# A retention and RWKV-7 backbone on one core: a second home for the retention heads' queries, values, decays and states

## The chip, the cores and the metric

The kernel runs on one core of one Trainium2 chip. What counts is the device time of one execution in microseconds, the median of several runs. The core has five engines that each take their instructions in a fixed order: TensorE (PE in the rows, its weight loads PEld), VectorE (DVE), ScalarE (ACT), GpSimd (POOL) and SyncE (SP), on whose queue this kernel issues its DMAs.

## What is computed

Two layers over 1024 latent and 256 context tokens of width 1024. Each layer normalises the tokens, makes one input projection, and splits its columns between eight retention heads and eight RWKV-7 heads of width 64. Both groups scan the tokens in both directions; the outputs are gated, joined, sent through one output projection and added to the residual. Cut to the retention heads, which the change touches:

```python
def retention_scan(q, k, v, log_gamma, s0):          # chunks of 128 tokens
    def step(s, qkv):
        qc, kc, vc = qkv
        scores = jnp.einsum('bhid,bhjd->bhij', qc, kc) * decay_mask
        inner = jnp.einsum('bhij,bhjd->bhid', scores, vc)
        cross = jnp.einsum('bhid,bhde->bhie', qc * q_decay, s)
        s_new = s * chunk_decay + jnp.einsum('bhjd,bhje->bhde', kc * k_decay, vc)
        return s_new, inner + cross
...
    mix_l = jnp.concatenate([ret_l * silu(gr_l), rwo_l * silu(gw_l)], axis=-1) @ w_out[layer]
```

## The kernel before

The 1280 tokens are ten tiles of 128 (`NT`). Heads are worked on in pairs, so there are four pairs (`NP`) of retention heads and four of RWKV heads in each of the two layers.

The RWKV heads set the pace. For each pair and each of ten steps, `prep` loads features from DRAM, `prep2` builds the small matrices of the step (L962 and L1001 to L1040), and `seq` carries the state on (L1053, L1061). `prep` runs `LOOK` = 3 steps and one ahead. `seq` and `prep2` are traced with high priority. The RWKV results of two tiles go through `readout`.

Everything else is filler, written as generators that yield after each piece of work, with its weight. `stream()` goes over the pairs. For pair p it merges `ret_out(p - 1)`, the retention output of the pair before, with `feats(p)`: the RWKV gates of pair p and the RWKV features of pair p + 1. Then come `ret_keys(p)` and `ret_states(p)`. For the last pair (3) there are no further features, and `ret_keys(3)` is itself part of `feats(3)`; so `ret_states(3)` follows on `ret_out(2)` directly. `out_stream()` then merges `ret_out(3)` with the retention gates of pair 3 and a first part of the output projection (`out_part`), and goes on with the second part, which needs the retention output of pair 3. After each step of the scan `deal` takes as much filler as a plan of weights (`DENSE`, `DUE`) says. This gives a program order. From it the compiler's planner makes the order on each engine: an instruction may be put ahead of earlier ones where its inputs, its buffers and its engine are free by the planner's estimate of times.

A projection (`project_steps`) goes over blocks of up to 512 tokens. For each block it takes one of two PSUM banks (`pj=2`), runs 24 products into it (L493 to L495, three for each of eight slices of the width, with weights and inputs split into two halves of 16 bits), and hands the bank to a sink that copies it out on ScalarE.

`ret_states(p)` projects the values (sink at L555: copies to tiles of the ring `ta`, five in all, transposes through the bank `fs`, copy to `vt` at L563), computes the decays `dec` (L581) and the mask `dmask` (L584, its inputs in the ring `tb`, four tiles), and projects the queries (sink at L551: copy to `qt` at L552, then the rotation `rope`, which also uses `ta`). Beside the queries it computes for each tile the state that it adds (`states`, in the single bank `rt`, L589 to L597) and copies it to `sbp` (L602), and then scans these (L618). For pairs 0 to 2 the retention gates follow (`ret_gates`, stored to `rgat_d` at L623). `ret_out(p)` then reads, tile pair by tile pair, in the bank `rt`: keys and queries (L638), queries and states (L641), mask (L643), decays (L644, L645), values (L648). Its `tail` normalises, loads the gates (L666) and stores the result to `mix_d`, which `mix_in` reads for the output projection (L809).

`qt`, `vt`, `dec`, `dmask` and the ten `sbp` tiles exist once in the pool `ret`: pair p writes them after pair p - 1 has read them. The keys `kt` of pairs 0 to 2 exist once too (`rk`); those of pair 3 lie in another pool (`pk`).

Of the kernel before, what the change touches and what calls it, by code (L numbers as in the profile page):

```python
# [10 lines left out]
F32 = mybir.dt.float32  # L11
# [11 lines left out]
TOK = SEQ + CTX  # L23
NT = TOK // 128
# [101 lines left out]
def hybrid_kernel(ctx: ExitStack, tc: tile.TileContext, a: dict, out: bass.AP, dbg: dict | None = None):  # L126
    nc = tc.nc
# [11 lines left out]
    def bank(tag, name):  # L139
        return ps.tile([128, 512], F32, tag=tag, name=name, bufs=BANKS[tag])  # L140
# [24 lines left out]
    def x_tile(tb):  # L165
        t = ln_pool.tile([128, D], F32, tag="xt", name="xt", bufs=XTB)
        load(t, a["ctx"][0, 128 * tb:128 * tb + 128, :] if tb < 2 else a["x"][0, 128 * (tb - 2):128 * (tb - 2) + 128, :])
        return t
# [86 lines left out]
    def t256(name, ring="ta"):  # L255
        pool = open_pools["ret"][1] if ring == "tb" else pre
        return pool.tile([128, 256], F32, tag=ring, name=name, bufs=dict(ta=TAB, tb=TBB)[ring])
# [76 lines left out]
            halves.append((hi, lo))  # L334
        return halves

    sbp = []
    SIDES = ("left", "right")


# [33 lines left out]
    for l in range(DEPTH):  # L374
# [55 lines left out]
        if l == 0:  # L430
            lp = ln_pool
            stage = [lp.tile([128, 8, 128 * len(tiles)], F32, name=f"xs{ci}") for ci, tiles in enumerate(LN_TILES)]
            for ci, tiles in enumerate(LN_TILES):
# [5 lines left out]
                for i, tb in enumerate(tiles):  # L439
                    t = x_tiles[tb] if tb < XTB else x_tile(tb)  # L440
# [40 lines left out]
        def project_steps(c0, pieces, sink):  # L481
            halves = w_block(w_in, c0)
            for piece in pieces:
                t0, t1 = piece[0], piece[1]
                m0, m1 = piece[2:] if len(piece) == 4 else (t0, t1)
                p = pj("pproj")
                n = m1 - m0
                for hf in range(2):
                    hi, lo = halves[hf]
                    for k in range(4):  # L490
                        kk = 4 * hf + k
                        first, stop = kk == 0, kk == 7
                        nc.tensor.matmul(p[:, 0:n], hi[:, k, :], h_hi[:, kk, m0:m1], start=first, stop=False)  # L493
                        nc.tensor.matmul(p[:, 0:n], hi[:, k, :], h_lo[:, kk, m0:m1], start=False, stop=False)  # L494
                        nc.tensor.matmul(p[:, 0:n], lo[:, k, :], h_hi[:, kk, m0:m1], start=False, stop=stop)  # L495
                sink(p, m0, t0, t1)
                yield 24 * (m1 - m0) / 2400
# [25 lines left out]
        def rope(x, t0, t1):  # L523
            if t0 < CTX:
                return
            for u in range(t0, t1, 256):
                cs, sn, sw = t256("ropec"), t256("ropes"), t256("rsw")
                load(cs, a["c_cos"][:, u - CTX:u - CTX + 256])
                load(sn, a["c_sin"][:, u - CTX:u - CTX + 256])
                xs = x[:, u - t0:u - t0 + 256]  # L530
                nc.vector.stream_shuffle(sw, xs, [(i + 16) % 32 for i in range(32)])
                nc.gpsimd.tensor_tensor(sw, sw, sn, ALU.mult)
                nc.vector.tensor_tensor(xs, xs, cs, ALU.mult)
                nc.vector.tensor_tensor(xs, xs, sw, ALU.add)
# [10 lines left out]

        def ret_states(rp, c):
            sp, kt = open_pools["ret"][1], c["kt"]
            qt = c["qt"] = sp.tile([128, TOK], F32, tag="qt", name="qt")
            vt = c["vt"] = sp.tile([128, NT, 128], F32, tag="vtk", name="vtk")

            def qsink(p, m0, t0, t1):  # L551
                nc.scalar.activation(qt[:, t0:t1], p[:, 0:t1 - t0], AF.Copy, scale=1.0 / WS)  # L552
                rope(qt[:, t0:t1], t0, t1)

            def vsink(p, m0, t0, t1):  # L555
                vch = [t256("vch") for _ in range(0, t1 - t0, 256)]
                for u, x in enumerate(vch):
                    nc.scalar.activation(x, p[:, 256 * u:256 * u + 256], AF.Copy, scale=1.0 / WS)
                p = bank("fs", "pvv")
                for u, x in enumerate(vch):  # L560
                    for j in range(2):
                        nc.tensor.transpose(p[:, 256 * u + 128 * j:256 * u + 128 * j + 128], x[:, 128 * j:128 * j + 128], ident)
                nc.scalar.copy(vt[:, t0 // 128:t1 // 128, :].rearrange("p g c -> p (g c)"), p[:, 0:t1 - t0])  # L563

            yield from project_steps(COL_V + 128 * rp, CHUNKS, vsink)


            dec = c["dec"] = sp.tile([128, 2, 2, 2], F32, tag="dec", name="dec")
            cd = sp.tile([128, 2], F32, tag="cd", name="cd")
            dmask = c["dmask"] = sp.tile([128, 2, 128], F32, tag="dmk", name="dmask")  # L570
            for d in range(2):
                nc.scalar.activation(cd[:, d:d + 1], lgc[:, 4 * d + rp:4 * d + rp + 1], AF.Exp, scale=128.0)
            rel, tri = [t256(nm, "tb").rearrange("p (d t) -> p d t", d=2) for nm in ("rel", "tri")]
            load(rel, a["c_rel"][:, 0:2])
            load(tri, a["c_rel"][:, 2:4])
            for hh in range(2):
                t2 = t256("dmt", "tb").rearrange("p (d t) -> p d t", d=2)
                for d in range(2):
                    col = lgb[:, 8 * d + 2 * rp + hh:8 * d + 2 * rp + hh + 1]
                    for w in range(2):  # L580
                        nc.scalar.activation(dec[:, w, d, hh:hh + 1], kdix[:, 2 * w + d:2 * w + d + 1], AF.Exp, scale=col)  # L581
                    nc.scalar.activation(t2[:, d, :], rel[:, d, :], AF.Exp, scale=col)
                nc.vector.tensor_tensor(t2, t2, tri, ALU.mult)
                nc.vector.tensor_tensor(dmask[:, hh, :], t2[:, 0, :], t2[:, 1, :], ALU.add)  # L584


            def states(j):
                pk = bank("rt", "pkt")
                nc.tensor.transpose(pk[:, 0:128], kt[:, 128 * j:128 * j + 128], ident)  # L589
                kk = t256("kkd", "tb").rearrange("p (d c) -> p d c", d=2)  # L590
                for d in range(2):
                    nc.vector.tensor_tensor(kk[:, d, :].rearrange("p (h c) -> p h c", h=2),
                                            pk[:, 0:128].rearrange("p (h c) -> p h c", h=2),
                                            dec[:, 0, d, :].unsqueeze(2).to_broadcast([128, 2, 64]), ALU.mult)
                for d in range(2):
                    for hh in range(2):
                        nc.tensor.matmul(pk[64 * hh:64 * hh + 64, 128 + 64 * d:192 + 64 * d], kk[:, d, 64 * hh:64 * hh + 64],  # L597
                                         vt[:, j, 64 * hh:64 * hh + 64], start=True, stop=True)
                for d in range(2):
                    i = order[d].index(j)  # L600
                    if i + 1 < NT:
                        nc.scalar.copy(sbp[order[d][i + 1]][:, 64 * d:64 * d + 64], pk[:, 128 + 64 * d:192 + 64 * d])  # L602

            def own_states():
                for j in range(NT):
                    states(j)
                    yield 0.43

            def queries():
                yield from project_steps(COL_Q + 128 * rp, lat_chunks, qsink)  # L610
                if rp < NP - 1:
                    yield from ret_gates(rp)

            yield from merge(own_states(), 4.3, queries(), 26)
            for d in range(2):
                for i in range(2, NT):
                    x = sbp[order[d][i]][:, 64 * d:64 * d + 64]
                    nc.vector.scalar_tensor_tensor(x, sbp[order[d][i - 1]][:, 64 * d:64 * d + 64], cd[:, d:d + 1], x,  # L618
                                                   ALU.mult, ALU.add)

        def ret_gates(rp):
            def gsink(p, m0, t0, t1):
                load(rgat_d[:, t0:t1], gate_of(p))  # L623

            yield from project_steps(COL_G + 128 * rp, [(128 * j, 128 * j + 256) for j in out_tiles[::2]], gsink)

        def ret_out(rp, c, pairs):
            sp = open_pools["ret"][1]
            kt, qt, vt, dec, dmask = [c[x] for x in ("kt", "qt", "vt", "dec", "dmask")]

            def inner(j0, hh, ob):

# [603 lines left out]
        sp = open_pool("scan", other)  # L1236
        make_rings(sp)
        rp = open_pool("ret", other)
        sbp[:] = [rp.tile([128, 128], F32, name=f"sbp{j}") for j in range(NT)]
        for j in range(NT):  # L1240
            nc.gpsimd.memset(sbp[j], 0.0)
        stages, late = {}, {}

        def ahead(g):
# [71 lines left out]
```

## Time and profile before

| | |
|---|---|
| median of 3 runs | 2458.19 us (2457.12 to 2461.14) |
| the profiled execution | 2462.74 us |
| its span, first to last instruction | 2460.7 us |
| mean granted TensorE clock | 0.964 of 2.4 GHz |
| TensorE busy | 2299.2 us (93%) |
| TensorE weight loads | 1739.9 us (71%) |
| VectorE, ScalarE, GpSimd busy | 1735.6, 1414.8, 1319.7 us |

Rows of the profile have the form: line of the kernel, engine, operation, output tile <- input tiles, shapes, count. Times are microseconds from the start of the span. The profile has views by line, by stretch of time, of waits, and in order of time. Matmuls are pipelined, so a busy TensorE isn't one at its peak.

### The profile page before, as it was taken

What the parts mean: (1) busy time and instruction counts of PE and PEld (TensorE: products, weight loads), DVE (VectorE), ACT (ScalarE), POOL (GpSimd) and SP (SyncE); (2) the same over time, 40 slices, a digit from 0 to 9 for tenths busy, and PEclk for the clock granted to TensorE, in tenths of its full rate; (3) what the DMA queues carried; (4) which work ended last, traced back from release to release, by engine and by line L of the source; (5) the groups of instructions that cost most, each with busy time, mean ns of one, the idle gap of its engine ahead of it and who ended that gap; (6) DMA issues with size and microseconds to landing.
All of it is one profiled execution on the core that took longest, in us unless ns stands there. A gap on an engine that the chain in (4) does not pass through costs nothing.

```text
span 2460.7 us, 69593 instructions
## 1 busy us (share of the span) xinstructions
PE 2299.2 (93%) x25463; PEld 1739.9 (71%) x25463; DVE 1735.6 (71%) x4784; ACT 1414.8 (57%) x4261; POOL 1319.7 (54%) x2032
## 2 busy tenths in 40 slices
PE   5779999999999999999997899999999999998997
PEld 2357776877788777778655687778768877776855
DVE  2646686787678867777648677767867886669756
ACT  3455664565566655456546666646655665456663
POOL 1455564465556654456536556545654665456662
PEclk7888999999999999999998899999999999999998
DMA  8754443334334423335533543434433443334544
GB/s 313 270 187 110 117 118 87 113 108 124 78 89 139 126 70 92 75 100 154 176 108 123 152 130 112 108 94 119 128 87 100 124 124 80 79 88 120 143 130 128
DMA packets 539606, 302.77 MB, mean 123 GB/s; under 512 B 238995, under 2 KB 526465, under 8 KB 537217
## 3 DMA queue, kind: packets, MB, share of 16 engines
q1 hardware_dynamic: 539264, 298.33, 42.1%
q8 instruction: 201, 3.29, 0.6%
q14 instruction: 141, 1.15, 0.2%
HBM read 212.21 MB, written 85.98 MB: 121 GB/s over the span
## 4 chain that ended last, share of the span: by engine, by line
PE 58%; DVE 13%; DMA 6%; ACT 4%; issue 3%; POOL 2%; SPq 2%; DVEq 0%; POOLq 0%; ACTq 0%
PE pproj L493 8%; PE pproj L495 8%; PE pproj L494 8%; PE pseq L1061 8%; PE pm L962 5%; DMA ft<-feat 2%; PE pseq L1053 2%; PE pinv L1001 2%; PE pinv L1017 2%; PE pout L821 1%; PE pout L823 1%; PE pss L638 1%; PE pout L822 1%; PE pss L648 1%; PE pyt L1127 1%
## 5 line engine op out<-in xcount | busy, mean ns | idle before, releaser
L493 PE MATMUL pproj<-h_hi,whi 128*128 128x256 f16 (+2 forms) x2128 | 631.3, 298 | 9.1 <-ACT craw L505 5.1
L494 PE MATMUL pproj<-h_lo,whi 128*128 128x256 f16 (+2 forms) x2128 | 629.1, 297 | 7.6 <-DVE h_lo L365 7.1
L495 PE MATMUL pproj<-h_hi,wlo 128*128 128x256 f16 (+2 forms) x2128 | 627.2, 297 | 0.7 <-POOL wlo L320 0.7
L320 POOL TENSOR_TENSOR wlo<-wraw,whi 128x256 f16<-128x256 f32 x360 | 250.5, 707 | 208.7 <-ACT wraw L319 181.0
L495 PEld LDWEIGHTS <-wlo 128*128 128x128 f16 x2128 | 213.5, 100 | 76.5 <-issue 12.1
L494 PEld LDWEIGHTS <-whi 128*128 128x128 f16 x2128 | 212.6, 100 | 77.6 <-issue 18.6
L493 PEld LDWEIGHTS <-whi 128*128 128x128 f16 x2128 | 213.1, 100 | 75.3 <-issue 10.4
L986 POOL COPY ttb<-tt 64x256 f16<-64x256 f16 x320 | 139.1, 436 | 205.2 <-DVE tt L1021 160.5
L1015 DVE TENSOR_TENSOR xx<-pinv,lvm 128x256 f16<-128x256 f32 x400 | 164.3, 416 | 90.6 <-PE pinv L1001 87.4
L318 ACT ACTIVATE whi<-wraw 128x256 f16<-128x256 f32 x360 | 139.2, 412 | 132.9 <-PE pproj L494 61.1
L1018 ACT CAST tz<-pinv 128x256 f16<-128x256 f32 x400 | 146.1, 370 | 119.9 <-PE pinv L1017 107.7
L962 PE MATMUL pm<-own,bk 64*128 64x128 f32 (+1 forms) x1280 | 201.6, 294 | 8.3 <-DVE bk L942 4.0
L1021 DVE STREAM_TRANSPOSE tt<-tz 128x256 f16<-128x256 f16 x320 | 139.4, 437 | 97.0 <-ACT tz L1018 94.3
L976 POOL TENSOR_TENSOR il<-gq,c_id 64x256 f32<-64x256 f32 x160 | 120.1, 751 | 133.1 <-DVE gq L965 119.3
L986 ACT COPY ttb<-tt 64x256 f16<-64x256 f16 x320 | 128.6, 402 | 106.5 <-DVE tt L1021 102.1
L962 PEld LDWEIGHTS pm<-own,bk 64*128 64x128 f32 x1280 | 163.2, 193 | 33.1 <-issue 8.6
L965 DVE TENSOR_TENSOR gq<-pm,c_m 128x256 f32<-128x256 f32 (+1 forms) x320 | 115.7, 402 | 50.6 <-PE pm L962 49.8
L1061 PE MATMUL pseq<-st,own 64*64 64x64 f32 x2432 | 149.4, 228 | 0.0
L319 ACT ACTIVATE wraw<-wraw 128x256 f32<-128x256 f32 x376 | 146.3, 410 | 3.9
L1001 PEld LDWEIGHTS <-hi 128*128 128x128 f16 x1920 | 104.6, 99 | 41.6 <-issue 9.7
L1012 POOL TENSOR_TENSOR lo<-il,hi 64x256 f16<-64x256 f32 x160 | 113.5, 710 | 36.8 <-ACT hi L977 28.0
L1008 POOL TENSOR_TENSOR ttb<-hi,lvm 128x256 f16<-128x256 f16 x160 | 113.6, 729 | 19.0 <-ACT hi L977 18.2
(255 smaller groups left out, 5906.7 us busy)
## 6 DMA issues: line engine op xcount, KB each, us to landing
ft<-feat SPq DMA_DIRECT2D x320, 160.0 KB
wraw<-in_w_in_dram SPq DMA_DIRECT2D x264, 128.0 KB
feat<-zth SPq DMA_DIRECT2D x80, 256.0 KB
wm<-in_w_mod_dram SPq DMA_DIRECT2D x16, 1024.0 KB
wraw<-in_w_out_dram SPq DMA_DIRECT2D x112, 128.0 KB
lap<-la SPq DMA_DIRECT2D x40, 256.0 KB
uv<-vt SPq DMA_DIRECT2D x320, 32.0 KB
wm<-in_w_mod_dram SPq DMA_DIRECT2D x16, 512.0 KB
```

The source lines that it names most:

```text
L319: nc.scalar.activation(raw, raw, AF.Copy, scale=WS)
L320: nc.gpsimd.tensor_tensor(lo, raw, hi, ALU.subtract)
L493: nc.tensor.matmul(p[:, 0:n], hi[:, k, :], h_hi[:, kk, m0:m1], start=first, stop=False)
L494: nc.tensor.matmul(p[:, 0:n], hi[:, k, :], h_lo[:, kk, m0:m1], start=False, stop=False)
L495: nc.tensor.matmul(p[:, 0:n], lo[:, k, :], h_hi[:, kk, m0:m1], start=False, stop=stop)
L962: nc.tensor.matmul(pm[h][:, i, d, 0:q1], bk[HR[h], i, d, :], own[HR[h], i, d, 0:q1], start=True, stop=True)
L986: eng(idr(dst[HR[h], :, :, 64 * h:64 * h + 64]), idr(src[HR[h]]))
L1001: nc.tensor.matmul(q[:, i, d, :], hi[:, i, d, :], id16 if n == 0 else tz[:, i, d, :], start=True, stop=True)
L1015: nc.vector.tensor_tensor(xx, q, mk, ALU.mult)
L1018: nc.scalar.copy(tzn, tp)
L1021: nc.vector.transpose(idr(tt), idr(tzn))
L1061: rm = nc.tensor.matmul(pq[HR[h], k, d, :], lhs, rhs, start=False, stop=stop, skip_group_check=True)
```

## The change

Queries, values, decays and mask get two buffers each, so that the pairs take them in turn. The ten state tiles are made twice, all twenty are set to zero at the start of a layer, and pair p uses set p % 2; `ret_out` gets its pair's set through the pair's dictionary `c`. Keys, the banks, the rings and the order in which the work is traced stay as they are.

```diff
-    sbp = []
+    sbps = []
...
-            qt = c["qt"] = sp.tile([128, TOK], F32, tag="qt", name="qt")
-            vt = c["vt"] = sp.tile([128, NT, 128], F32, tag="vtk", name="vtk")
+
+            sbp = c["sbp"] = sbps[rp % 2]
+            qt = c["qt"] = sp.tile([128, TOK], F32, tag="qt", name="qt", bufs=2)
+            vt = c["vt"] = sp.tile([128, NT, 128], F32, tag="vtk", name="vtk", bufs=2)
...
-            dec = c["dec"] = sp.tile([128, 2, 2, 2], F32, tag="dec", name="dec")
+            dec = c["dec"] = sp.tile([128, 2, 2, 2], F32, tag="dec", name="dec", bufs=2)
             cd = sp.tile([128, 2], F32, tag="cd", name="cd")
-            dmask = c["dmask"] = sp.tile([128, 2, 128], F32, tag="dmk", name="dmask")
+            dmask = c["dmask"] = sp.tile([128, 2, 128], F32, tag="dmk", name="dmask", bufs=2)
...
-            kt, qt, vt, dec, dmask = [c[x] for x in ("kt", "qt", "vt", "dec", "dmask")]
+            kt, qt, vt, dec, dmask, sbp = [c[x] for x in ("kt", "qt", "vt", "dec", "dmask", "sbp")]
...
-        sbp[:] = [rp.tile([128, 128], F32, name=f"sbp{j}") for j in range(NT)]
-        for j in range(NT):
-            nc.gpsimd.memset(sbp[j], 0.0)
+        sbps[:] = [[rp.tile([128, 128], F32, name=f"sbp{n}{j}") for j in range(NT)] for n in range(2)]
+        for t in sbps[0] + sbps[1]:
+            nc.gpsimd.memset(t, 0.0)
```

## Rows read from the trace of the kernel before

**Rows 1.** The page: busy time of each engine, and the chain's shares by engine.
```profile
PE 2299.2 (93%) x25463; PEld 1739.9 (71%) x25463; DVE 1735.6 (71%) x4784; ACT 1414.8 (57%) x4261; POOL 1319.7 (54%) x2032
...
PE 58%; DVE 13%; DMA 6%; ACT 4%; issue 3%; POOL 2%; SPq 2%; DVEq 0%; POOLq 0%; ACTq 0%
```

**Rows 2.** L493 alone by window: length, busy and count, clock, DMA share, GB/s.
```profile
1000.00:1019.50 19.50, 5.90 (x18) 1.76 (x18) 1.00 0.36 89
1020.40:1053.90 33.50, 0.00 (x0) 0.00 (x0) 0.75 0.28 74
...
2181.40:2198.70 17.30, 0.07 (x1) 0.00 (x0) 0.76 0.30 77
...
2211.50:2227.50 16.00, 0.00 (x0) 0.16 (x1) 0.70 0.39 104
```

**Rows 3.** All engines by window: PE, PEld, DVE, ACT, POOL, granted clock, DMA.
```profile
1020.40:1036.80 16.40, 14.67 (x212) 12.28 (x210) 14.36 (x47) 9.28 (x27) 8.77 (x14) 1.00 0.36 93
1036.80:1057.30 20.50, 20.05 (x156) 15.52 (x157) 11.57 (x32) 8.73 (x32) 7.66 (x13) 0.50 0.16 46
2181.60:2190.50 8.90, 7.31 (x100) 6.05 (x99) 7.17 (x20) 5.15 (x14) 7.17 (x12) 1.00 0.29 77
2190.50:2200.80 10.30, 10.14 (x95) 8.56 (x95) 7.88 (x31) 5.19 (x16) 3.37 (x7) 0.50 0.30 75
2211.60:2217.80 6.20, 4.83 (x63) 3.82 (x61) 5.74 (x21) 4.12 (x12) 2.65 (x4) 1.00 0.50 157
2217.80:2228.10 10.30, 6.59 (x72) 4.88 (x69) 10.13 (x30) 4.36 (x16) 5.74 (x8) 0.50 0.34 78
```

**Rows 4.** ScalarE in order of time: start, length, instruction, idle before it.
```profile
1050.51 0.38 ACT L552 ACTIVATE qt<-pproj 128x256 f32<-128x256 f32 x1 [2.12 <-PE pss L641]
...
1061.96 0.37 ACT L563 COPY vtk<-pvv 128x256 f32<-128x256 f32 x1
...
2196.84 0.60 ACT L552 ACTIVATE qt<-pproj 128x512 f32<-128x512 f32 x1 [1.73 <-PE pss L641]
...
2220.97 0.38 ACT L686 ACTIVATE gth<-pproj 128x256 f32<-128x256 f32 x1 [0.41 <-DVE qt L533]
```

**Rows 5.** TensorE in order of time, around the same places.
```profile
1020.46 0.38 PE L495 MATMUL pproj<-h_hi,wlo 128*128 128x512 f16 x1
...
1049.42 1.06 PE L641 MATMUL pss<-sbp,qt 64*128 64x128 f32 x4
...
1053.99 0.61 PE L493 MATMUL pproj<-h_hi,whi 128*128 128x512 f16 x1
...
1061.29 0.64 PE L648 MATMUL pss<-vtk,smk 128*128 128x64 f32 x4
...
2181.52 0.38 PE L495 MATMUL pproj<-h_hi,wlo 128*128 128x512 f16 x1
...
2195.75 1.06 PE L641 MATMUL pss<-sbp,qt 64*128 64x128 f32 x4
```

**Rows 6.** Pairs 0 and 1 of layer 0, in order of time.
```profile
570.99 0.61 PE L641 MATMUL pss<-sbp,qt 64*128 64x128 f32 x4
...
635.72 0.38 ACT L552 ACTIVATE qt<-pproj 128x256 f32<-128x256 f32 x1
```

**Rows 7.** GpSimd in order of time, at the start of each layer's scan.
```profile
149.94 1.50 POOL L1241 MEMSET sbp<- 128x128 f32 x8
...
1299.16 1.54 POOL L1241 MEMSET sbp<- 128x128 f32 x10 [4.67 <-PE pout L823]
```

**Rows 8.** SyncE's DMA issues in order of time: gate reads, gate store, first mix load.
```profile
1031.35 0.58 SPq L666 DMA_DIRECT2D rmx<-rgat  x1
...
1049.36 0.53 SPq L666 DMA_DIRECT2D rmx<-rgat  x1
...
2242.40 0.38 SPq L623 DMA_DIRECT2D rgat<-gs  x1
2242.88 2.30 SPq L809 DMA_DIRECT2D mraw<-mix  x5
```

## The prediction

> **What bounds the kernel now.** I read the page's busy line and its chain first [rows 1]. In both TensorE leads: 93% of the span in its row, 58% of the chain, with the three product lines of the projections (L493, L494, L495) at the head of the chain's list. The other engines lie at 54 to 71%. So the kernel ends when TensorE has got through its work, and the question for any edit is whether TensorE is at some point short of work, or slow, because of what the edit touches.
>
> What TensorE does is of two kinds. The RWKV chain (`prep2` and `seq`) is a row of short, dependent products. The filler is projections and output products, dealt between the chain's steps. So I next asked for the filler alone: L493, the first of each three products, window by window [rows 2]. Ordinarily 18 of them start in 19.5 us. In three places none do: 33.5 us in layer 0 (1020.4 to 1053.9), 17.3 us in layer 1 (2181.4 on; the one that is counted is the end of an earlier one), and 16.0 us a little later (2211.5 on). In the whole of these windows only the RWKV chain and the retention output run.
>
> Third, all engines in the same places with the granted clock [rows 3]. In layer 0 the clock is still 1.00 in the first 16.4 us without filler, then 0.50 (1.2 instead of 2.4 GHz) for 20.5 us, until just after the filler is back. In layer 1 it is 0.50 for 10.3 us twice, again in the two lulls. Together 41.1 us at the lower level. TensorE's idle time in these windows is 16.40 - 14.67 + 20.50 - 20.05 = 2.2 us in layer 0, and 1.59 + 0.16 + 1.37 + 3.71 = 6.8 us in layer 1.
>
> The page "Perfetto Trace Analysis" of the Trainium skill (Identifying the Most-Contended Engine) says that the matmul busy share is a bad measure of what TensorE has left. The trace agrees: the row with 20.05 of 20.50 us busy holds 156 matmuls, the 16.40 us ahead of it 212 [rows 3]. By the busy share alone the lulls hold 9.0 us; with the clock it is three times that.
>
> Last, who ends the lulls [rows 4, 5]. In layer 0 the last product of the second query block of pair 3 starts at 1020.46. ScalarE copies the pair's query blocks out of PSUM (L552) only at 1050.51, and its idle time is put down to `PE pss L641`, the last product that reads the queries of pair 2 (1049.42 + 1.06 us). Two blocks wait so, and the projections have two PSUM banks (`pj=2`): no projection can start. L493 is back at 1053.99. For the values it is the same: last reader L648 at 1061.29, first copy L563 at 1061.96. In layer 1: the last query product at 2181.52, the reader at 2195.75, the copy at 2196.84. The second lull of layer 1 follows from that: the first gate block is taken up (L686) only at 2220.97, behind a `DVE qt L533`, the rotation of the late queries.
>
> It happens only with pair 3 of each layer. For pairs 1 and 2 `ret_keys` lies between (pair 3 does its keys earlier): the last read of pair 0's queries is at 570.99, pair 1's copy at 635.72, 64 us later with nothing waiting [rows 6]. Pair 2 is alike.
>
> **The change, part by part.**
>
> Queries, two homes: takes the wait of L552 away. Pair 3 takes the home that pair 1 left long ago. The two banks come free as soon as their products end (the later one at about 1021) instead of at 1051. What can then follow is the third query block (layer 0 only) and the gates of pair 3, five blocks in layer 0, four in layer 1: 6 x 8 = 48 and 4 x 8 = 32 products on L493. At the usual 18 in 19.5 us they would last 52 and 35 us; many are 256 columns wide and not 512, so half of that is the lower bound: 26 to 52 us for a lull of 33.5, and 17 to 35 us for lulls of 33.3 together.
>
> Values, two homes: L563 needn't wait for L648. Alone it opens little (the five value tiles in front of it find room), but it frees the `ta` tiles that the query rotation and the gates need next.
>
> What that is worth: the busy time at half clock would halve, (20.05 + 10.14 + 6.59) / 2 = 18.4 us, and the idle time is 9.0 us: 27.4 us at most. At least nothing, if the hole only moves. I take two thirds, 18.3 us, since the filler just about covers the lulls. What is late next: the first loads for the output products (L809, 2242.88) start right behind the last gate store (2242.40) [rows 8], so they too come forward, until they meet the end of `ret_out` of pair 2.
>
> States, decays and mask, two homes: nothing. States of the next pair can't start before `ret_out` of the last pair is done, for both use the one `rt` bank in turn, and the mask's inputs turn in the shared `tb` tiles. Only a few ScalarE exponentials on single columns (L581) may come earlier; they hide beside TensorE.
>
> Ten more memsets on GpSimd per layer: ten took 1.54 us in a row in layer 1, and eight 1.50 us in layer 0 [rows 7], so 1.5 us each layer. Behind them are `zth` and the normalisation of layer 1. Zero if hidden, 3.0 us if not; I take 1.5.
>
> The planner orders all instructions anew by its own estimates of time, and the pool grows by 16.4 KB per partition (5,120 bytes each for queries, values and states, 1,056 for mask and decays). What a new order costs elsewhere no row of before shows. The nearest are the lulls themselves: one more or one less like the shorter ones is 10.14 / 2 + 1.6 = 6.7 us either way. I take zero and keep both ends for the range.
>
> Sum: -18.3 + 1.5 = -17 us. The profiled execution took 2462.7 us (2460.7 of span and 2.0 around it), so 2446 for its like; the median of the three runs lies 4.5 us lower, at 2458.19. Forecast: 2441.
>
> **The rivals.**
>
> The clock stays low anyway. It doesn't fall for want of filler; or the moved filler is spread so thinly that it falls all the same. For it: in the half-clock stretch TensorE is already busy 20.05 of 20.50 us. Against: in three lulls of three the clock falls within the lull and is back with the filler. Then only idle time comes back, 9.0 x 2/3 - 3.0 = 3 us: 2455 (2450 to 2458). The page "TensorE: Matmul & The Clock Gate" of the Trainium skill (Part 1: The HAM clock gate) ties the lower clock to an idle engine; by that rule the lull of layer 0, busy in its row, would not be its cause. The rows bear it out only in part.
>
> The hole moves. Filler that is spent at 1020 to 1054 is missing later, ahead of the last output part, which needs the retention output of pair 3, and that isn't earlier. Then the same lull comes once more, and with memsets it is 2458 to 2461; I write 2460. Against: RWKV steps run ahead in a lull, so only their last stretch is lost.
>
> Slower, by SyncE's queue. The gates' stores (L623) overwrite the ranges that `ret_out` of pair 2 still reads (L666). Brought forward, a store must wait for its read, and behind it on SyncE's queue are `ft` and `uv`, the loads of the next RWKV step. The reads are 18 us apart (1031.35, 1049.36) [rows 8]. If the planner takes these reads for earlier than they are, one such wait per layer that outlasts the steps prepared ahead costs up to 18 us; half of it, in a layer or spread over both, makes 2458 + 9, so 2468 with the memsets. It decides when a wait outlasts the steps that are prepared ahead (LOOK is 3). Against: that is a long cover.
>
> Better than the forecast: lulls gone entirely, and the output parts packed more tightly: below 2431.
>
> **How the numbers follow.** Forecast 2441 with 2431 to 2449: 0.52. Better: 0.06. Clock stays low: 0.14. Hole moves: 0.12. Slower: 0.16. About 0.2% is what can be told from no change (2453.3 to 2463.1). Faster by more: 0.52 + 0.06 + 0.06 of the second = 0.64. Within: 0.08 + 0.10 = 0.18. Slower: 0.02 + 0.16 = 0.18. The range goes from 2428 to 2468: it takes in the slower rival's price and one spare lull below the forecast.
>
> **What would show it.** Right: L552 of pair 3 within 2 us of its products in both layers; L493 present in each 20 us between 1000 and 1075 and between 2160 and 2220; no half clock there; the first output products some 20 us earlier against the RWKV steps. The memsets show as 20 of L1241's kind a layer. Wrong, if L552 is prompt and a stretch of half clock stands somewhere else in the same layer, or if `ft` lands late behind an L623 store.

## The result: slower by 0.8%

| | before | after |
|---|---|---|
| median of 6 runs each | 2462.86 us (2457.12 to 2466.58) | 2482.76 us (2474.55 to 2489.18) |
| the profiled execution | 2462.74 us | 2484.52 us |
| its span | 2460.7 us | 2482.7 us |
| mean granted TensorE clock | 0.964 | 0.958 |
| time at the lower clock, summed over the span | 178.0 us | 210.4 us |
| TensorE busy | 2299.2 us | 2318.0 us |

The ratio is 1.008 [1.0055, 1.0104]: the change costs 20 us. The forecast was 2441, the range ended at 2468. TensorE executes the same 25463 matmuls and counts as busy 18.8 us longer; it spends 32.4 us more at the lower clock. Both are of one execution each, and neither is the price of the change, as two kernels further down show.

The page after, busy line and chain by engine, against [rows 1]. Below, lines of the kernel after carry numbers two higher than before, from L552 (now L554) on.

```profile
PE 2318.0 (93%) x25463; PEld 1750.8 (71%) x25463; DVE 1715.1 (69%) x4784; ACT 1419.2 (57%) x4261; POOL 1327.1 (53%) x2052
...
PE 68%; DVE 10%; DMA 5%; ACT 4%; issue 3%; POOL 2%; SPq 1%; DVEq 0%; POOLq 0%; ACTq 0%
```

**What the change was to do, it did.** ScalarE after, in order of time, against [rows 4]: the value copy of pair 3, its three query copies in layer 0 and the two in layer 1.

```profile
983.87 0.37 ACT L565 COPY vtk<-pvv 128x256 f32<-128x256 f32 x1 [0.67 <-PE pvv L564]
1007.29 0.38 ACT L554 ACTIVATE qt<-pproj 128x256 f32<-128x256 f32 x1 [0.60 <-PE pproj L495]
1019.86 0.60 ACT L554 ACTIVATE qt<-pproj 128x512 f32<-128x512 f32 x1
1030.05 0.58 ACT L554 ACTIVATE qt<-pproj 128x512 f32<-128x512 f32 x1
...
2187.69 0.60 ACT L554 ACTIVATE qt<-pproj 128x512 f32<-128x512 f32 x1 [0.42 <-PE pproj L495]
2196.71 0.58 ACT L554 ACTIVATE qt<-pproj 128x512 f32<-128x512 f32 x1
```

None of these copies has a read of pair 2's queries (`pss`) as its releaser any more, and the first one of layer 0 is 43 us earlier than 1050.51. L493 alone in the same places, against [rows 2] (length, busy and count, weight loads, clock, DMA share, GB/s):

```profile
1000.00:1020.00 20.00, 5.22 (x16) 1.62 (x16) 1.00 0.40 99
1020.00:1068.50 48.50, 13.24 (x47) 4.55 (x46) 1.00 0.36 93
1069.50:1180.00 110.50, 0.00 (x0) 0.00 (x0) 0.91 0.46 123
2181.40:2198.70 17.30, 6.22 (x18) 1.67 (x18) 1.00 0.43 108
2198.80:2222.50 23.70, 6.89 (x26) 2.59 (x26) 1.00 0.31 87
```

The lulls are gone, and the clock is 1.00 where it was 0.75, 0.76 and 0.70. The third row says what became of it: the layer's projections are used up by 1068.9, where before they last until 1095.7. From then on the output part is the only filler, beside the retention work itself.

**Where it was given back.** First, right behind. The output part starts at 1071.0 instead of 1098.2, and as slowly as before (there 9 of the first of each three products in its first 17 us). The first of each three output products after, by window:

```profile
1069.50:1094.70 25.20, 3.04 (x8) 1.12 (x9) 0.66 0.43 123
```

Second, ahead of the second output part. TensorE after, then SyncE and ScalarE, in order of time: the first own state of pair 3 (L591), the last product of the first output part, the last read-out of pair 3's retention output (L666), the first product of the second output part; the loads of the second part's first three inputs (L811) and pair 3's last store (L670); the copies that turn these inputs into the 16-bit tiles `mh` for the products (L813).

```profile
1076.13 0.47 PE L591 MATMUL pkt<-c_id,kt 128*128 128x128 f32 x1
...
1186.75 0.27 PE L825 MATMUL pout<-mh,wlo 128*128 128x256 f16 x1
...
1203.34 0.69 PE L666 MATMUL pot<-c_id,ob 128*128 128x128 f32 x2
...
1208.30 0.40 PE L823 MATMUL pout<-mh,whi 128*128 128x256 f16 x1
```
```profile
1105.38 1.37 SPq L811 DMA_DIRECT2D mraw<-mix  x3
...
1205.24 0.33 SPq L670 DMA_DIRECT2D mix<-rmx  x1
```
```profile
1207.10 1.02 ACT L813 CAST mh<-mraw 128x256 f16<-128x256 f32 x3 [1.03 <-DMA mix<-rmx]
```

Pair 3's states need the `rt` bank, which `ret_out(2)` holds until about 1075: 1076.13 now, 1074.3 before. So its retention output ends no earlier (last read-out at 1203.3 against 1192.1), and its last store is issued at 1205.24.

The second part waits for that store, but not for its data. Pair 3's output is only one of the seven or eight blocks that a sum of the second part adds up, and the three inputs that are copied at 1207.10 were loaded from 1105.38 on, before the first of pair 3's results was stored (1164.23). The copy waits all the same on the semaphores of pair 3's last three stores (1187.99, 1197.46, 1205.24). These read tiles `rmx` of the ring `tb`, in the pool `ret`; and in the program the pool of `mh` is opened after `ret` has been closed. So what is left is memory: `mh` has been given a place that `ret` still holds. Before, the same copy goes long before the last store:

```profile
1138.50 0.41 ACT L811 CAST mh<-mraw 128x256 f16<-128x256 f32 x1
...
1194.04 0.46 SPq L668 DMA_DIRECT2D mix<-rmx  x1
```

All the traces of this study divide so, in layer 0 (the kernels are described below):

| kernels | `ret` larger by, bytes per partition | first copy of the second part against pair 3's last store | largest gap in the filler, 1100 to 1300 |
|---|---|---|---|
| queries and values twice, 7 | 10,240 to 16,416 | 1.8 to 3.1 us after it | 19 to 31 us |
| the same, with a bank of their own, 4 | 22,560 | 2.0 to 3.2 us after it | 7.1 to 7.9 us |
| the other 7, before among them | 0 to 6,176 | 51 to 75 us before it | 3.5 to 9.1 us |

`e4_v` shows that a late retention output alone makes no such gap: its last store is later than the change's, yet a product of the second part (in layer 0 only that part has products 512 columns wide) goes 7.8 us ahead of it, and no gap is over 6.7 us.

```profile
1202.16 0.38 PE L823 MATMUL pout<-mh,whi 128*128 128x512 f16 x1
...
1209.95 0.58 SPq L670 DMA_DIRECT2D mix<-rmx  x1
```

That the size of the pool is what decides is argued from the table: no kernel has a larger pool and nothing else, and no trace shows where the tiles lie.

The projections that might have been done meanwhile were done by 1068.9. From 1186.75 to 1208.30, 21.6 us, no filler of any kind starts. Before, the largest such gap was 6.0 us. The first of each three output products by window, after and then before:

```profile
1100.00:1186.70 86.70, 23.19 (x84) 8.42 (x84) 0.98 0.44 120
1186.80:1208.20 21.40, 0.00 (x0) 0.00 (x0) 0.90 0.59 204
...
2417.40:2432.80 15.40, 0.00 (x0) 0.13 (x1) 0.78 0.71 189
```
```profile
1187.00:1208.00 21.00, 8.59 (x30) 2.94 (x30) 1.00 0.64 190
...
2416.00:2432.00 16.00, 3.46 (x11) 1.38 (x11) 0.92 0.48 137
```

And the clock, all engines after, by window (PE, PEld, DVE, ACT, POOL, clock, DMA), against [rows 3]: the place of the old lull first, then the new ones.

```profile
1040.00:1074.00 34.00, 31.50 (x414) 26.29 (x411) 27.39 (x77) 20.36 (x62) 20.50 (x33) 1.00 0.35 94
1074.30:1084.50 10.20, 9.54 (x110) 7.49 (x110) 9.32 (x35) 5.57 (x21) 5.14 (x11) 0.50 0.39 113
1084.50:1094.70 10.20, 8.47 (x92) 6.71 (x91) 5.85 (x19) 5.51 (x19) 2.21 (x4) 0.67 0.43 119
1200.00:1224.40 24.40, 20.08 (x232) 13.67 (x231) 14.79 (x52) 12.18 (x38) 8.26 (x14) 0.79 0.39 117
...
2417.20:2433.00 15.80, 10.91 (x189) 8.51 (x188) 9.93 (x35) 7.00 (x21) 4.64 (x8) 0.78 0.69 185
2425.90:2436.10 10.20, 7.92 (x91) 5.76 (x89) 4.91 (x19) 3.97 (x12) 0.40 (x1) 0.50 0.35 95
```

The stretch at 0.50 that stood at 1036.8 to 1057.3 stands at 1074.3 to 1094.7, less deep, and again at 1200 to 1224. Late in layer 1 a new lull lies ahead of the last output part, 15.8 us from 2417.2, which had no counterpart over 5.0 us. After 230 us the kernel before spends 96.1 us at the lower clock, the kernel after 138.7, 43 us more. That sum doesn't price the loss: `e5_dec` has 136.0 us and its time can't be told from that of before, `e1_qv` has 103.6 us and loses 1.3%.

**The two traces at equal work.** Clock times can't be compared once the order differs, so I weighed each matmul by the usual spacing of its form in the kernel before (the lower quartile of the times from its start to the next one's), and asked at what time each kernel had done the same share of the whole. The difference to before, gained or lost within each stretch (stretches by the time of before; us; one profiled execution each, so single microseconds carry nothing; weighed by the median spacing instead, single stretches move by up to some 7 us, and those of the change to -12.5, +24.9 and -4.6 where the table has -15.7, +28.1 and -6.6). All kernels of this study stand here; their edits follow below.

```
stretch of before  4-1000 1000-1080 1080-1320 1320-1560 1560-2160 2160-2210 2210-2400 2400-end  total
after                -4.7     -15.7     +28.1     +10.3      -3.2      -6.6      +1.5    +12.4  +22.0
queries and values freed
 e1_qv               -1.2     -16.0     +21.2      +1.8      -1.5      -8.6      +2.1    +18.9  +16.6
 e9_qv_dec           -4.2     -16.0     +28.0      +0.9      -3.8      -6.5      -3.3    +12.2   +7.4
 e10_qv_few          -1.9     -16.0     +25.9      +5.8      +1.6      -8.6       0.0    +15.0  +21.9
 e7_fewmem           -3.7     -16.0     +25.9      +9.8      -5.2      -7.6      -5.1    +14.1  +12.1
 e13_after_due       -3.9     -16.0     +32.5      -1.8      -7.2      -5.6      -1.0    +12.3   +9.3
 e16_qvdec_due       -6.8     -15.7     +29.4     +10.1      -4.3      -7.6      +3.4    +17.5  +26.1
and the states of pair 3 in a bank of their own
 e8_ownbank          +8.6     -14.0     +10.0      +6.5      +0.5      -5.8      -8.2    +14.7  +12.3
 e11_bank_few        +7.9     -14.1     +17.3      +7.3      -2.5      -5.8      -9.0    +14.6  +15.8
 e12_bank_retw       +8.2     -14.0     +21.2      +7.6      +1.5      -5.8     -10.1    +16.6  +25.3
 e15_bank_due        +9.2     -14.1     +20.8      +3.5      -6.7      -6.2     -10.6    +12.3   +8.2
one of the two freed
 e2_q                -1.9      -1.4     +24.7      +1.9      +1.0      -2.3      +7.0    +12.3  +41.5
 e4_v                +0.9      -6.0      +2.6      +1.3      -4.3      +7.0      -9.2    +14.4   +6.7
neither freed
 e3_s                -4.7      -0.9      +8.0      +3.8      +0.7      +0.8      +0.3    +13.1  +21.2
 e5_dec              -5.3      -0.9      +7.7      -0.5      -2.6      -4.0      -1.3    +12.9   +6.0
 e6_few              -1.5      +0.6      +0.9      +1.7      -4.2      -3.9      +7.7     +4.4   +5.8
 e14_before_due      -1.6      -8.1      +0.3      +4.3      -5.9      -3.9      +4.3    +14.8   +4.1
```

The row "after" has the predicted gain, 15.7 us in layer 0 and 6.6 in layer 1; 28.1 us go right behind it; 10.3 go around the layers' border and 12.4 at the end. In finer stretches the 28.1 are 13.7 between 1080 and 1100, where the kernel before still has projections, and 18.3 between 1200 and 1220, the gap; 9.9 come back between 1240 and 1280, probably because RWKV steps ran ahead in the gap (12.0, 10.5 and 3.1 with the median spacings).

### The profile page after: what moved, and what is told of

It reads as the page before. It is cut to its first block, busy times and chain, and to the rows that moved or that the text cites. A ratio compares the mean times of both kernels' runs of the same rounds, so it can differ in the third digit from the quotient of the medians.

```text
span 2482.7 us, 69586 instructions
## 1 busy us (share of the span) xinstructions
PE 2318.0 (93%) x25463; PEld 1750.8 (71%) x25463; DVE 1715.1 (69%) x4784; ACT 1419.2 (57%) x4261; POOL 1327.1 (53%) x2052
## 4 chain that ended last, share of the span: by engine, by line
PE 68%; DVE 10%; DMA 5%; ACT 4%; issue 3%; POOL 2%; SPq 1%; DVEq 0%; POOLq 0%; ACTq 0%
PE pproj L495 9%; PE pproj L493 9%; PE pproj L494 9%; PE pseq L1063 9%; PE pm L964 6%; PE pinv L1003 2%; PE pseq L1055 2%; PE pout L823 2%; PE pout L825 2%; PE pinv L1019 2%; PE pout L824 2%; PE pss L640 1%; DMA ft<-feat 1%; PE pss L643 1%; PE pss L650 1%
## 5 line engine op out<-in xcount | busy, mean ns | idle before, releaser
L493 PE MATMUL pproj<-h_hi,whi 128*128 128x256 f16 (+2 forms) x2128 | 631.3, 298 | 13.9 <-ACT craw L505 6.6
L493 PEld LDWEIGHTS <-whi 128*128 128x128 f16 x2128 | 212.9, 100 | 78.1 <-issue 13.0
L1019 PE MATMUL pinv<-xx,ttb 128*128 128x64 f16 x1600 | 115.7, 196 | 8.7 <-DVE xx L1017 7.4
```

The lines of the kernel that those rows point to most:

```text
L1019: nc.tensor.matmul(tp[:, i, d, :], ttb[:, i, d, :], xx[:, i, d, :], start=True, stop=True)
```

## The experiments

Three explanations were on trial. First, that the hole moves: freed queries and values spend the filler early, and the output part behind pair 3 then waits. Second, the ten more memsets at the layers' border. Third, that the planner lays out the whole kernel anew after any such edit, and the new order is worse for reasons that have nothing to do with the freed homes. That the larger pool makes the second output part wait wasn't on trial; every edit that frees both queries and values also enlarges the pool by 10,240 bytes or more.

**Which part of the change costs.** From the kernel before, only some of the second homes; the ten memsets a layer stay unless noted.

`e1_qv`, queries and values alone:
```diff
-qt = ... tag="qt", name="qt")
-vt = ... tag="vtk", name="vtk")
+qt = ... tag="qt", name="qt", bufs=2)
+vt = ... tag="vtk", name="vtk", bufs=2)
```


> Only queries and values have two homes; states, decays, mask and the memsets stay as before. Theory 1 (the filler that is freed comes forward, and the lull with its half clock moves behind it, to the wait for the output parts and to the end of each layer): most of the loss is here, +12 to +24 us against the kernel before, pair 3's query copies prompt, at least 15 us of half clock between 1060 and 1240 us. Theory 2 (the ten more memsets and the larger pool delay the start of each layer's scan): within 5 us of before. Theory 3 (any edit makes the planner lay out another order, and the loss is chance): anywhere between -10 and +25 us.

Measured: 2486.77 us, 1.0132 [1.0100, 1.0165]. The loss is there without any second state set, mask, decay or added memset, and with it the gap behind pair 3: 28.5 us without an output product from 1176 on, longer than with the whole change. The loss is above the range of either theory that expected one.

`e2_q`, the first of these two edits (`qt`) alone.

> Only the queries have two homes. Theory 1: the two projection banks come free, so the filler comes forward as in the full change; +8 to +24 us against the kernel before. The values still wait, so the rotation of the queries and the gates find fewer tiles of the ring ta and the filler comes less far forward. Theory 2: within 5 us. Theory 3: anywhere between -10 and +25 us.

Measured: 2504.86 us, 1.0205 [1.0184, 1.0226], the slowest of all, and twice the most that any theory gave. With one home the values wait as before, until the last product on pair 2's values is done. ScalarE's first value copy, L493 alone, and all engines a little later:

```profile
1060.46 0.37 ACT L565 COPY vtk<-pvv 128x256 f32<-128x256 f32 x1
```
```profile
1045.60:1087.00 41.40, 0.00 (x0) 0.00 (x0) 0.63 0.38 99
```
```profile
1056.40:1090.50 34.10, 31.20 (x282) 25.52 (x282) 27.68 (x93) 16.37 (x54) 15.85 (x26) 0.50 0.41 105
```

The lull isn't shorter but longer, 41.4 us against 33.5, and the clock is low for 34.1 us against 20.5. Freed alone, the queries let the filler run on to 1045.6, where it meets the next wait in line.

`e4_v`, the second edit (`vt`) alone.

> Only the values have two homes. Theory 1: the query copies still wait, and both banks with them, so the lull stays, 25 to 34 us in layer 0; within 6 us of before. Theory 2: within 5 us. Theory 3: anywhere between -10 and +25 us.

Measured: 2467.48 us, 1.0039 [1.0012, 1.0066], a small loss. The lull stays, 29.9 us long in layer 0; as the prediction's step on the values has it, they open little alone (-6.0 us in 1000 to 1080).

`e3_s`, the other half of the change: states, decays and mask twice, with twenty memsets; queries and values once.
```diff
-dec = ... tag="dec", name="dec")
+dec = ... tag="dec", name="dec", bufs=2)
-dmask = ... tag="dmk", name="dmask")
+dmask = ... tag="dmk", name="dmask", bufs=2)
+sbp = c["sbp"] = sbps[rp % 2]
```


> Queries and values have one home as before; states, decays and mask have two, with the ten more memsets per layer. Theory 1: the lull before the query copies of pair 3 is there as before, 30 us long in layer 0 with some 20 us at half clock, and the time is within 6 us of before. Theory 2: +15 to +22 us, and the step after the layer's change starts 10 us or more later than before. Theory 3: anywhere between -10 and +25 us.

Measured: 2472.52 us, 1.0076 [1.0043, 1.0109]. The lull is where it was, nothing is gained there, there is no gap behind pair 3 (largest 5.4 us), and yet it is 0.8% slower. So the first explanation isn't the whole one.

**How much a new order alone costs.** Edits that free no filler. Two homes for the decays alone are enough for a new order: on TensorE it departs from that of before at 170.6 us.

`e5_dec`, only the decays twice.
```diff
-dec = ... tag="dec", name="dec")
+dec = ... tag="dec", name="dec", bufs=2)
```


> The kernel before with two homes for the decays alone, eight columns of one number per partition. No wait of the profile hangs on them, so the lull before the query copies of pair 3 must be there as before. Theory 1 (the loss comes from filler that the freed queries bring forward): within 4 us of before. Theory 3 (any edit that changes a dependency makes the planner lay out another order, and the order of before is an unusually good one): +4 to +18 us, without any filler brought forward in pair 3, and spread over places that have nothing to do with the decays.

Measured: 2464.23 us, 1.0011 [0.9988, 1.0033], so no difference that can be told. Within it, 7.7 us go behind 1080 and 12.9 at the end, and come back in smaller sums elsewhere.

`e6_few`, the kernel before, with two memsets a layer instead of ten (it leaves out the zeroing of the other eight state tiles).
```diff
-        for j in range(NT):
+        for j in range(2):
             nc.gpsimd.memset(sbp[j], 0.0)
```


> The kernel before with eight memsets fewer per layer: only the two state tiles that are read without having been written are set to zero. Less work on GpSimd, one home for everything. Theory 1: within 4 us of before, at most 3 us faster. Theory 3: +4 to +18 us although there is less work.

Measured: 2463.67 us, 1.0025 [1.0003, 1.0046]. Less work, and if anything slower.

`e7_fewmem`, the changed kernel with four memsets a layer instead of twenty (two of each set; the others are left out).
```diff
-        for t in sbps[0] + sbps[1]:
+        for t in sbps[0][0:2] + sbps[1][0:2]:
```

> The changed kernel with four memsets per layer instead of twenty, so without the memsets that the change added. Theory 2 (the added memsets and their wait at the start of layer 1 cost some 10 us at the change of layers): 8 to 14 us faster than the changed kernel, +6 to +12 us against before. Theory 1: within 4 us of the changed kernel (+15 to +24 us against before). Theory 3: anywhere from +4 to +25 us against before.

Measured: 2472.30 us, 1.0058 [1.0036, 1.0080] against 1.0080 [1.0055, 1.0104] for the change: the intervals overlap. The stretch around the layers' border still loses 9.8 us of 10.3. So the added memsets carry a part of the loss at most; that stretch goes from -1.8 to +10.3 over the orders of the table, and what sets it isn't settled.

`e9_qv_dec` (queries, values and decays twice) and `e10_qv_few` (queries and values twice, two memsets a layer, the others left out) repeat `e1_qv` in the company of `e5_dec` and `e6_few`.

> Queries, values and decays have two homes, the states one, memsets as before. It stands to the kernel with decays alone (+0.11%) as queries and values alone (+1.32%) stand to the kernel before. Theory 1 (freeing queries and values in pair 3 is a loss by itself, since the filler is spent ahead of the wait for pair 3's states): +0.6% or more above the kernel with decays alone, so +15 to +35 us against before. Theory 3 (all differences are the planner's chance): as likely below that kernel as above it.

> Queries and values have two homes, the states one, with two memsets per layer. It stands to the kernel with fewer memsets alone (+0.25%) as queries and values alone (+1.32%) stand to the kernel before. Theory 1: +0.6% or more above the kernel with fewer memsets alone, so +20 to +38 us against before. Theory 3: as likely below that kernel as above it.

Measured: 2473.01 us, 1.0068 [1.0041, 1.0095], and 2483.40 us, 1.0103 [1.0078, 1.0128]. With them freeing can be read four times, each time with the rest alike:

| the rest | queries and values once | twice | freeing them |
|---|---|---|---|
| as before | 1 | 1.0132 | +1.3% |
| decays twice | 1.0011 | 1.0068 | +0.6% |
| two memsets | 1.0025 | 1.0103 | +0.8% |
| states, decays, mask twice | 1.0076 | 1.0080 | 0.0% |

It never gains; the mean is +0.7%, some 17 us. The spread, 0.0 to 1.3%, says that the same edit is worth different amounts in different company; that the planner's order makes the difference is likely and not shown. So neither half has a price that could be added to the other's: 1.3% and 0.8% make 0.8% together. Each "twice" also has a pool that is larger by 10,240 bytes, so the freed wait and the memory that it takes haven't been tried apart. An unused tile of that size in the kernel before, or the second output part's tiles in a place that `ret` never has, would do it; neither was run.

**Is it the `rt` bank that holds pair 3's output back?** `e8_ownbank`: the changed kernel, with the states of pair 3 in bank `fs`, and their inputs and those of the mask in rings of their own (of its edit, two lines).
```diff
-                pk = bank("rt", "pkt")
+                pk = bank("fs" if rp == NP - 1 else "rt", "pkt")
-                kk = t256("kkd", "tb")...
+                kk = t256("kkd", "tk" if rp == NP - 1 else "tb")...
```


> The changed kernel, in which the states of pair 3 get a PSUM bank (fs instead of rt) and tiles (two for the keys, four for the mask's inputs) of their own, so that they need not wait for the retention output of pair 2. Theory 1 (the freed filler is spent while the states of pair 3 still wait for that output, and the second output part then waits for pair 3): the first transposes of pair 3's states start 30 us earlier or more in layer 0 (by about 1040 us instead of 1076), the gap of 21 us in the output products ahead of their second part shrinks to under 10 us, and the time is 8 to 25 us below that of the changed kernel, -5 to +12 us against before. Theory 3: the states come earlier too, but the time stays between +4 and +25 us against before.

Measured: 2479.39 us, 1.0096 [1.0062, 1.0129]. TensorE, the first own state of pair 3; pair 3's last store and the first copy of the second part's inputs; and the first of each three output products by window:

```profile
1030.16 0.28 PE L591 MATMUL pkt<-c_id,kt 128*128 128x128 f32 x1
```
```profile
1179.89 0.53 SPq L670 DMA_DIRECT2D mix<-rmx  x1
...
1181.85 1.02 ACT L813 CAST mh<-mraw 128x256 f16<-128x256 f32 x3
```
```profile
1100.00:1187.00 87.00, 21.39 (x79) 7.83 (x79) 1.00 0.47 129
1187.00:1208.00 21.00, 6.44 (x23) 2.25 (x23) 1.00 0.65 204
```

The states start 46 us earlier, and the gap is gone: 23 products where there were none, at clock 1.00, largest gap 7.1 us. From 1000 to 1320 this kernel is 4.0 us ahead of before (0.2 with the median spacings, which stand in brackets here), where the change is 12.4 behind. That shows the chain, for bank and rings together: states, retention output, last store, release of the pool, second output part. The gap isn't what most of the difference comes from: 12.4 us (10.5) of it lie between 1080 and 1100, where this kernel still has projections, until 1087.7. And the time isn't better, for 8.6 us (4.7) are lost before 1000, where the bank of pair 3 plays no part, and 14.7 at the end. `e11_bank_few` (with four memsets a layer, the others left out) and `e12_bank_retw` (besides, `RETW = 16` for 32, which is to take the retention output of pair 3 twice as fast against the gates and the first output part that it is merged with) vary it:
```diff
-RETW = 32
+RETW = 16
```

> The changed kernel with four memsets per layer and with a bank and tiles of their own for the states of pair 3. Theory 1: in layer 0, between 1000 and 1320 us of the kernel before, it wins what the changed kernel lost there (12 us), as the first kernel with the own bank did; +0 to +18 us against before in all, since the end of the kernel isn't touched. Theory 3: +4 to +30 us, and no gain in that stretch.

> As the last one, and RETW is 16 instead of 32: the retention output of pair 3 stands earlier in the program order against the first output part, so that the second output part can begin sooner. Theory 1: the second output part starts 10 us earlier or more against the end of the first, and the time is 3 to 15 us below that of the last one (-10 to +12 us against before). Theory 3: anywhere between -5 and +30 us.

Measured: 2482.41 us, 1.0099 [1.0070, 1.0127], and 2480.49 us, 1.0087 [1.0056, 1.0117]. From 1000 to 1320 they stand at +3.2 and +7.2, so the 4.0 us gained by `e8_ownbank` doesn't hold either; over its four kernels the own bank leaves +3.3 us on average there (+7.2), against +11.4 in the seven with queries and values freed and the shared bank. `RETW` didn't do its part: pair 3's last store comes at 1184.5, with 32 at 1180.7. The gap goes; a net gain doesn't come.

**The end of layer 1.** In every new order but that of `e6_few` 12 to 19 us go after 2400, and a gap of some 13 to 20 us stands ahead of the last output part (before: 5.0; `e6_few`: 4.2). Two readings: the filler is used up too early by the plan, or the order of before is a lucky one. The plan's last due step, made one step later, should close the gap by the first:
```diff
-DUE = (30, 37)
+DUE = (30, 38)
```
`e13_after_due` has it in the changed kernel, `e14_before_due` in the kernel before, `e15_bank_due` in `e11_bank_few`, `e16_qvdec_due` in `e9_qv_dec`.

> The changed kernel with DUE = (30, 38) instead of (30, 37): the output parts of each layer are dealt out by step 38 and not by 37. Theory 1 (the end is lost because the filler is used up before the last part can start): the gap in the output products ahead of the last part, 16 us in layer 1, shrinks to under 8 us, and the time is 4 to 14 us below the changed kernel's (+6 to +18 us against before). Theory 3 (the order of before is a lucky one): gap and time as in the changed kernel, +14 to +30 us.

> The kernel before with DUE = (30, 38). Theory 1: its filler lasts to the end already, so a later plan only defers work: 0 to +12 us. Theory 3: a new order, +3 to +18 us, with a gap of 10 us or more ahead of the last output part.

> The changed kernel with four memsets per layer, a bank and tiles of their own for the states of pair 3, and DUE = (30, 38). Theory 1: 4 to 14 us below the same without the later plan (so +8 to +22 us against before). Theory 3: +14 to +32 us.

> Queries, values and decays with two homes, and DUE = (30, 38). Theory 1: 4 to 14 us below the same without the later plan (so +2 to +13 us against before). Theory 3: +8 to +28 us.

Measured: 2470.12 us, 1.0049 [1.0025, 1.0073]; 2466.22, 1.0033 [1.0009, 1.0057]; 2472.45, 1.0057 [1.0037, 1.0077]; 2485.17, 1.0104 [1.0065, 1.0142]. The first of each three output products in the gap, `e13_after_due` and then `e14_before_due`:

```profile
2407.80:2420.50 12.70, 0.00 (x0) 0.00 (x0) 0.63 0.79 203
```
```profile
2398.50:2414.30 15.80, 0.00 (x0) 0.10 (x1) 0.89 0.69 184
```

The gap stays, 13.2, 16.2, 14.7 and 19.5 us long, and the kernel before gets one of its own by an edit that frees nothing. The times of the first and third lie 0.3 and 0.4% below those of the kernels that they vary, as the first reading wanted, and that of the fourth 0.4% above; but the intervals overlap each time, and with the gap still there it isn't the gap that gave the times. So the first reading fell. What makes the order of before (and of `e6_few`) pack its last 60 us better isn't settled; no trace shows the planner's own estimates.

## Why the prediction was wrong

- **What bounds the kernel, and what the lulls cost:** right. With the wait gone the lulls filled, the clock stayed at 1.00 there, and the forecast gain of 18.3 us (27.4 at most) measured 15.7 + 6.6 = 22.3 us, or 17.1 with the median spacings.
- **Values opening little alone:** right (`e4_v`). That the queries alone would only meet the values' wait, I hadn't seen (`e2_q`).
- **"What is late next", and the larger pool:** the step that failed. It let the output part come forward "until they meet the end of `ret_out` of pair 2", and counted nothing for what comes after. The first part did come forward, by 27 us, and 13.7 us were lost at once between 1080 and 1100, where the projections had run out. The second part couldn't follow: its first copies waited until 1207.10 for the pool `ret`, and left 21.6 us bare. The prediction states that this pool grows by 16.4 KB, puts it beside the planner's order and takes zero for both.
- **The rival "the hole moves"** told this with its place, for a reason that holds in part: pair 3's retention output isn't earlier, but what waits for its last store is the memory. It was priced at 2460 and 0.12, because "RWKV steps run ahead in a lull, so only their last stretch is lost". The steps did run ahead: step 39, the last of layer 0, began at 1234.7 instead of 1259.7, and some of it came back. Even so the price measured 28.1 us between 1080 and 1320, more than the gain, and the first step of layer 1 began at 1441.7 instead of 1425.3.
- **The planner's new order, "zero, plus or minus 6.7 us":** mis-sized too, by its middle. `e5_dec`, `e6_few` and `e14_before_due` (which alters the plan itself), with no filler freed, measured +0.1 to +0.3%, 3 to 8 us; `e3_s`, half of the change itself, +0.8% or 19 us. None came out faster, though the first can't be told from before. At the end of layer 1 the loss of 12 us or more stands in every new order but one.
- **The memsets, 1.5 us:** not separable. GpSimd after takes twenty in 2.98 us in layer 1:

```profile
1354.28 2.98 POOL L1243 MEMSET sbp<- 128x128 f32 x20
```

  twice the 1.54 us for ten [rows 7], but the 10.3 us lost at the border don't go with them (`e7_fewmem`).
- **The rival on SyncE's queue:** its wait is there, but small: one gate store (L625) waits 2.6 us for the read of its range, between 1000 and 1064, and the engines' idle time for `ft` between 1000 and 1110 is 1.4 us. The forecast's own test, "wrong, if L552 is prompt and a stretch of half clock stands somewhere else in the same layer", is what came.

The page "Perfetto Trace Analysis" of the Trainium skill (Identifying Performance Opportunities, Optimization Strategy) says that a gap which repeats on the engine that should be saturated can mean too little room for the next tile, the number of buffers among it. The trace agrees as to the cause, the lulls of [rows 2] went with the second buffers; and the gap of 21.6 us that came with them, though a single one, is by the wait of the copy at 1207.10 again one of room for the next tile. It doesn't follow that the time goes with the lulls: it rose by 0.8%.

What share of the 20 us each cause has stays open: order, freed homes and the size of the pool weren't varied apart from one another, and the losses at the layers' border and at the end have no cause shown.

## What to carry to other kernels

A second buffer takes away a wait and takes memory. Ask both questions before it is made. Filler that fills one hole is missing at the next wait: follow the dependence on to the next place where the same engine will want that filler, and ask whether what it waits for there also comes earlier. And ask which tiles were laid in the memory that the buffer now takes: in a trace it shows as a first write to a new pool that waits for the last reader of an old one. Where a compiler's planner orders the instructions, run two or three edits that change a buffer without touching the wait in question beside the one meant: their spread (here up to 0.3%, none of them clearly faster) is the smallest effect that can be put down to the edit's own mechanism. Compare two orders at equal work and not at equal time; the stretch in which a gain is given back is then plain.

## What was not expected of the hardware

TensorE's granted clock stayed at the lower level while the engine counted as busy, for longer than in [rows 3]: 0.50 (1.2 of 2.4 GHz) for 34.1 us in `e2_q`, of which 31.20 us were busy with 282 matmuls, in a stretch in which no projection starts from 1045.6 to 1087. In 34.0 us at clock 1.00 in the kernel after (1040 to 1074) 31.50 us were busy, with 414.
